# A two-layer hybrid trunk in float32: branch and output products as pairs of 512 and 256 columns, in a written order

## The chip, the cores and the metric

The kernel runs on one core of one Trainium2 chip. A core has a matrix engine (PE, with a row of its own, PEld, for loading weights), a vector engine (DVE), a scalar engine (ACT), a general engine (POOL) and a queue engine (SP) that here only starts transfers. PE writes its products to PSUM, a memory of eight banks; DVE and ACT read PSUM, POOL does not. The metric is the time on the device for one execution, in microseconds (us). Three timed runs of the kernel before took 999.44 us in the median (999.4 to 999.6). What a measurement of this kernel can tell from no change is about 0.2%, or 2 us.

## The reference

One sequence of 256 positions and 1024 channels goes through two layers. All arrays are float32.

```
x = x + 0.5 * swiglu(rms_norm(x), ...)              # first FFN, hidden width 2816
h = rms_norm(x);  z = h @ w_in                       # u | q | k | v | gates
y_pool = per-group map of (causal window means of u minus u) * scale
y_attn = causal attention over q, k, v (one block of 256 positions)
gates  = sigmoid(gl + b_gate)                        # two gates per output channel
merged = gates[0] * (y_pool @ w_branch_pool) + gates[1] * (y_attn @ w_branch_attn)
x = x + merged @ w_out
x = x + 0.5 * swiglu(rms_norm(x), ...)              # second FFN
```

The change concerns the last lines of the middle part: the two **branch** products, the gated sum `merged`, the **output** product with `w_out`, the sum into `x`, and what the second FFN needs of the new `x`.

## The kernel before, in words

**Exact products.** Every float32 operand is split into a high part, rounded to the matrix engine's float32r format, and a low part, the rest. A product is the sum of three: high by high, high by low, low by high. A weight block of 128 by 128 meets an activation tile of 128 channels by 256 positions, held as its two parts side by side (2 x 256 columns). There are two ways to write a block:

- `chain` (a **pair**): the high weights meet both parts in one product of 512 columns, then the low weights meet the high part in one product of 256 columns, added onto the first half. The result has two halves of 256 columns in PSUM, which must be added afterwards.
- `chain3` (a **triple**): three products of 256 columns, all added in the same 256 columns of PSUM. Nothing is left to add.

**Weights.** They stream from memory in units of 1 MB (two halves of 128 x 1024). SP starts a unit's transfer into one of four raw buffers; for each half ACT copies the raw data to `hi` (line 122) and DVE subtracts to get `lo` (line 123). There are six buffers each for `hi` and `lo`, so three units may stand ready. `request()` issues one whole unit, and `unit()` hands out the next.

**The middle of a layer.** After attention and the last two gate pairs, PE computes 64 branch blocks (eight output groups f of 128 channels, for each four blocks of the pooled branch and four of the attention branch), then 64 output blocks (eight groups of eight), then goes straight on with the second FFN. In the branch part, `mixed(f)` multiplies the two branch sums by the gates, adds them and splits the result `mg` into the parts `mk[f]` that the output product reads. Groups f = 2, 3, 4 (the set `wide`) are pairs: ACT copies each second half out of PSUM and DVE adds the first half to it, four instructions for the two branches, and POOL makes the sum of the two branches. The other five groups are triples, and DVE reads their PSUM tile directly. In the output part, groups 0 to 3 are pairs: ACT copies the second half, POOL adds `x`, DVE adds the first half. Groups 4 to 7 are triples with a single DVE addition. The output part starts groups 0, 1, 2 on the first six `mk`, then adds the last two.

**After each output group.** `after(f)` calls `prep`: ACT and DVE split the new `x` times a gain into `hx[f]`, the input parts of the second FFN, and ACT squares `x`, which DVE sums in `acc` for the norm. PE's first products of the FFN read `hx[0]`, `hx[1]` and so on. A little later PE sums `acc` over the channels with two products by ones (`ss`), for which `acc` is first split into `ar`.

**What sets the order.** Each engine runs its own instructions strictly in the order of its list, and waits in place. A scheduler of the framework writes these lists when the program is built. Instructions passed through `keep` stay in the order in which the code has them; PE's all are. DVE's and ACT's in the branch and output parts are not, so there the scheduler chose their order.

**The end.** The last FFN's last output group (22 blocks) is all triples, so that only one DVE instruction (line 451) stands between the last product and the last store.

Of the kernel before, what the change touches and what calls it, by code (L numbers as in the profile page):

```python
# [24 lines left out]
P = 128  # L25
D = 1024
S = 256
# [22 lines left out]
def trunk_kernel(ctx: ExitStack, tc: tile.TileContext, x_in, w_in, pw_in, qkn_in, rope_in, mask_in, band_in, out):  # L50
# [182 lines left out]
    nc.gpsimd.memset(uT[:, :, :PAD], 0.0)  # L233
# [8 lines left out]
    keep(nc.gpsimd.dma_start(gx[:, L * NG + 2 * S:L * NG + 4 * S], x_in[:, L * NG + 2 * S:L * NG + 4 * S]))  # L242

# [19 lines left out]
    def prep(f, l, col):  # L263
        split_x(f, l, col)
        square_x(f)
# [45 lines left out]
    def ffn(after, n0=0, end=False):  # L311
# [52 lines left out]
        for b in range(NK * NF):  # L364
# [5 lines left out]
            if f < NK - 1 or not end:  # L370
                chain(ps, hi, lo, b % 16, gs[k], k == 0, k == NF - 1)
            else:
                chain3(ps[:, 0, :], hi, lo, b % 16, gs[k:k + 1], k == 0, k == NF - 1)
# [71 lines left out]
    def add_x(f, ps, two):  # L445
# [120 lines left out]
    def mix(l, after):  # L566
# [26 lines left out]
        def open_gate(f):  # L593
            tt(gates[:, f], gates[:, f], bc2(r), op=OP.mult)
            for j in range(2):
                c = j * NK + f
                act(gates[:, f, j, :], gates[:, f, j, :], AF.Tanh, scale=0.5, bias=hb[:, c:c + 1])
# [137 lines left out]
        gate(7)  # L735
        open_gate(7)
        mt = acts.tile([P, NK, 2, S], F32R, name="mk", tag="ga")
        mk = [mt[:, i] for i in range(NK)]

        def branch(f, j, k0=0, k1=4):  # L740
            if f not in sums:
                sums[f] = quarter("two")
            if f in wide:
                for k in range(k0, k1):
                    chain(sums[f][j], *ws[f // 2], f % 2 * 8 + j * 4 + k, (pk, yk)[j][k], k == 0, k == 3)
            else:
                chain3(sums[f][:, j], *ws[f // 2], f % 2 * 8 + j * 4 + k0, (pk, yk)[j][k0:k1], k0 == j == 0,
                       j == 1 and k1 == 4)

        def mixed(f):  # L750
            mg = tmp.tile([P, 2, S], F32, name="mg", tag="t512", bufs=5)
            both = sums[f]
            if f in wide:
                both = mg
                for i in range(2):
                    act(mg[:, i, :], sums[f][i][:, 1, :], AF.Copy)
                    tt(mg[:, i, :], sums[f][i][:, 0, :], mg[:, i, :], op=OP.add)
            stt(mg, gates[:, f], 1.0, both, op0=OP.add, op1=OP.mult)
            (nc.gpsimd.tensor_tensor if f in wide else tt)(mg[:, 0, :], mg[:, 0, :], mg[:, 1, :], op=OP.add)
            halves(mk[f], mg[:, 0, :])  # L760

        ws = [unit() for _ in range(2)]
        sums = {f: quarter("two") for f in range(2)}
        wide = range(2, 5)
        sums.update({f: banks(pmm, "two") for f in range(2, 4)})
        sums = {f: [z[:, j] for j in range(2)] if f in wide else z for f, z in sums.items()}
        sums[4] = [quarter("two") for _ in range(2)]
        for f in range(4):
            for j in range(2):
                branch(f, j, 0, 2)  # L770
        for f in range(4):
            for j in range(2):
                branch(f, j, 2)
            mixed(f)
        for f in range(4, NK):
            if f % 2 == 0:
                ws.append(unit())
            for j in range(2):
                branch(f, j)
            mixed(f)  # L780
        ws, sums = [], []

        def project(f, k0=0, k1=NK):
# [5 lines left out]
            if f >= 4:  # L789
                chain3(ps[:, 0], *ws[f // 2], f % 2 * 8 + k0, mk[k0:k1], k0 == 0, k1 == NK)  # L790
            else:
                for k in range(k0, k1):
                    chain(ps, *ws[f // 2], f % 2 * 8 + k, mk[k], k == 0, k == NK - 1)
# [141 lines left out]
```

## Time and profile before

| | us |
|---|---|
| median of three timed runs | 999.44 |
| profiled execution, its own time | 999.57 |
| span of the profiled execution | 997.6 |
| PE, DVE, ACT, POOL busy | 993.6, 799.5, 628.7, 17.5 |
| branch part of layer 1, layer 2 (start to start of the output part) | 280.00 to 301.90, 774.1 to 796.0 |

The span covers all work that the profile shows; 2.0 us of the profiled execution's time lie around it. Each view below is of that one execution. In a timeline a row gives start, duration, engine, source line, operation, the tile that is written and the tiles that are read, the shape, how many like it follow at once, and in brackets how long the engine had been idle and what released it. On DVE and ACT an instruction may start some 0.08 us before the one ahead of it has ended, so the distance from start to start is what a row of instructions costs.

### The profile page before, as it was taken

What the parts mean: (1) busy time and instruction counts of PE and PEld (TensorE: products, weight loads), DVE (VectorE), ACT (ScalarE), POOL (GpSimd) and SP (SyncE); (2) the same over time, 40 slices, a digit from 0 to 9 for tenths busy, and PEclk for the clock granted to TensorE, in tenths of its full rate; (3) what the DMA queues carried; (4) which work ended last, traced back from release to release, by engine and by line L of the source; (5) the groups of instructions that cost most, each with busy time, mean ns of one, the idle gap of its engine ahead of it and who ended that gap; (6) DMA issues with size and microseconds to landing.
All of it is one profiled execution on the core that took longest, in us unless ns stands there. A gap on an engine that the chain in (4) does not pass through costs nothing.

```text
span 997.6 us, 15761 instructions
## 1 busy us (share of the span) xinstructions
PE 993.6 (100%) x6220; PEld 899.1 (90%) x6220; DVE 799.5 (80%) x1183; ACT 628.7 (63%) x999; POOL 17.5 (2%) x53
## 2 busy tenths in 40 slices
PE   9999999999999999999999999999999999999998
PEld 8998888898899988988898898888989999889888
DVE  7987786799879988886688888667998799888752
ACT  7766565657866766655576666556678567656541
POOL 1000000000001000000000000000000010000000
PEclk9999999999999999999999999999999999999999
DMA  9655565643536655655556566555545266555640
GB/s 314 243 207 209 194 245 214 220 170 120 219 127 211 214 208 182 204 207 204 181 193 215 178 211 205 182 204 191 193 151 194 100 235 216 198 204 189 211 143 27
DMA packets 30154, 192.88 MB, mean 193 GB/s; under 512 B 3360, under 2 KB 5408, under 8 KB 7552
## 3 DMA queue, kind: packets, MB, share of 16 engines
q1 hardware_dynamic: 29664, 191.18, 55.0%
q8 instruction: 48, 0.79, 0.3%
q0 software_dynamic: 128, 0.39, 0.1%
q10 hardware_dynamic: 288, 0.31, 0.1%
q14 instruction: 26, 0.21, 0.1%
HBM read 190.82 MB, written 1.05 MB: 192 GB/s over the span
## 4 chain that ended last, share of the span: by engine, by line
PE 100%; DVE 0%; issue 0%
PE ps L80 85%; PE pt L80 6%; PE two L80 4%; PE at L80 2%; PE pe L80 1%; PE at L546 1%; PE busy L80 0%; PE tp L507 0%; PE ss L80 0%; DVE gx L451 0%
## 5 line engine op out<-in xcount | busy, mean ns | idle before, releaser
L80 PE MATMUL ps<-hx,hi 128*128 128x512 f32 (+1 forms) x1714 | 572.2, 383 | 0.0
L123 DVE TENSOR_TENSOR lo<-raw,hi 128x1024 fp32r<-128x1024 f32 (+2 forms) x333 | 393.9, 1189 | 115.3 <-ACT hi L122 110.6
L80 PE MATMUL ps<-hx,lo 128*128 128x256 f32 x1712 | 464.6, 273 | 0.0
L122 ACT ACTIVATE hi<-raw 128x1024 fp32r<-128x1024 f32 (+2 forms) x333 | 339.6, 1029 | 190.4 <-PE ps L80 153.9
L80 PEld LDWEIGHTS ps<-hx,hi 128*128 128x128 f32 x1714 | 321.1, 188 | 56.8 <-issue 0.3
L80 PEld LDWEIGHTS ps<-hx,lo 128*128 128x128 f32 x1712 | 321.2, 188 | 0.8
L80 PE MATMUL ps<-ga,hi 128*128 128x512 f32 (+1 forms) x264 | 87.0, 376 | 0.0
L80 PE MATMUL ps<-gc,hi 128*128 128x512 f32 (+1 forms) x264 | 87.0, 376 | 0.0
L80 PE MATMUL ps<-ga,lo 128*128 128x256 f32 x256 | 69.9, 273 | 0.0
L80 PE MATMUL ps<-gc,lo 128*128 128x256 f32 x256 | 69.9, 273 | 0.0
L80 PE MATMUL ps<-gb,hi 128*128 128x512 f32 (+1 forms) x198 | 65.6, 376 | 0.0
L80 PE MATMUL pt<-hi,hx 128*128 128x512 f32 x192 | 64.3, 382 | 0.0
L80 PEld LDWEIGHTS ps<-ga,hi 128*128 128x128 f32 x264 | 49.0, 188 | 8.3
L80 PEld LDWEIGHTS ps<-gc,hi 128*128 128x128 f32 x264 | 49.0, 188 | 8.3
L80 PE MATMUL pt<-lo,hx 128*128 128x256 f32 x192 | 52.5, 273 | 0.0
L80 PE MATMUL ps<-gb,lo 128*128 128x256 f32 x192 | 52.4, 273 | 0.0
L190 DVE TENSOR_TENSOR ab<-ps,ab 128x512 f32<-128x512 f32 x56 | 38.6, 688 | 16.2 <-ACT ab L189 14.9
L80 PEld LDWEIGHTS ps<-ga,lo 128*128 128x128 f32 x256 | 48.1, 188 | 0.0
L80 PEld LDWEIGHTS ps<-gc,lo 128*128 128x128 f32 x256 | 48.1, 188 | 0.0
L388 DVE TENSOR_TENSOR lo<-raw,hi 128x1024 fp32r<-128x1024 f32 x38 | 44.7, 1217 | 0.0
L80 PE MATMUL two<-yp,hi 128*128 128x256 f32 (+1 forms) x208 | 43.9, 301 | 0.0
L80 PE MATMUL ps<-mk,hi 128*128 128x256 f32 (+1 forms) x192 | 43.5, 311 | 0.0
(162 smaller groups left out, 1130.1 us busy)
## 6 DMA issues: line engine op xcount, KB each, us to landing
raw<-w SPq DMA_DIRECT2D x176, 1024.0 KB, 4.9
raw<-w SPq DMA_DIRECT2D x6, 256.0 KB, 6.0
raw<-w SPq DMA_DIRECT2D x11, 128.0 KB, 3.8
raw<-w SPq DMA_DIRECT2D x2, 512.0 KB, 6.1
gx<-x SPq DMA_DIRECT2D x2, 256.0 KB, 5.7
qk<-pw SPq DMA_DIRECT2D x2, 256.0 KB, 3.3
out_dram<-gx SPq DMA_DIRECT2D x2, 256.0 KB, 2.7
out_dram<-gx SPq DMA_DIRECT2D x1, 384.0 KB, 5.4
```

What stands on the lines that cost most here:

```text
L80: return keep(nc.tensor.matmul(*args, **kw))
L122: put(act(hi, w, AF.Copy))
L123: put(tt(lo, w, hi.bitcast(F32), op=OP.subtract))
L190: put(tt(t, ps[:, :, 0, :], t, op=OP.add))
L388: keep(tt(lo[h], raw[:, h * HALF:(h + 1) * HALF], hi[h].bitcast(F32), op=OP.subtract))
L546: keep(nc.tensor.transpose(line(pt)[:, j * P:(j + 1) * P], pr[:, h, c * P:(c + 1) * P], ident))
```

## The change

1. All 64 branch blocks and all 64 output blocks are pairs. `branch` and the set `wide` are gone. For every group two PSUM tiles are taken, alternately from the two pools. ACT copies two second halves, DVE adds two first halves, and the sum of the two branches, before on POOL for three groups, is on DVE for all eight.
2. In the output part every group has ACT copy the second half, DVE add the first half to `x`, and DVE add the copy. POOL's four additions per layer are gone.
3. The order of ACT and DVE in these parts is written out with `keep`, `prep` included. Weights are split half a unit at a time by `next_half()`: after branch groups 0, 1, 2, 4 and 6, three halves after the last group, one half after each of output groups 0 to 5, and two at the end. Three units are requested ahead, behind the last gate pair's products.
4. The last gate pair is drained at once, but its scaling and its two activations (`open_gate(7)`) come after branch group 3.
5. The last group of the last FFN has 17 blocks as pairs in one PSUM tile, which is added to `x` with the usual three instructions (`add_x`), and five blocks as triples in a second tile, added with one.
6. The padding columns of `uT` are cleared one column at a time, on POOL, behind POOL's second input transfer instead of ahead of it.

```diff
-    nc.gpsimd.memset(uT[:, :, :PAD], 0.0)
...
+    for t in range(PAD):
+        keep(nc.gpsimd.memset(uT[:, :, t:t + 1], 0.0))
...
             if f < NK - 1 or not end:
                 chain(ps, hi, lo, b % 16, gs[k], k == 0, k == NF - 1)
+            elif k < NF - 5:
+                chain(ps, hi, lo, b % 16, gs[k], k == 0, k == NF - 6)
             else:
-                chain3(ps[:, 0, :], hi, lo, b % 16, gs[k:k + 1], k == 0, k == NF - 1)
+                if k == NF - 5:
+                    add_x(f, ps)
+                    ps = quarter("ps")
+                chain3(ps[:, 0, :], hi, lo, b % 16, gs[k:k + 1], k == NF - 5, k == NF - 1)
...
+        def next_half():
+
+            if not begun:
+                raw = raws.tile([P, 2 * HALF], F32, name="raw", tag="raw")
+                nc.sync.dma_start(raw, w_in[n_unit[0]])
+                n_unit[0] += 1
+                begun.append((raw, [], []))
+            raw, hi, lo = begun[0]
+            h = len(hi)
+            hi.append(parts.tile([P, HALF], F32R, name="hi", tag="hi"))
+            lo.append(parts.tile([P, HALF], F32R, name="lo", tag="lo"))
+            split(raw[:, h * HALF:(h + 1) * HALF], hi[h], lo[h], keep)
+            if h:
+                begun.clear()
+                ahead.append((hi, lo))
...
+        def mixed(f, ps):
+
             mg = tmp.tile([P, 2, S], F32, name="mg", tag="t512", bufs=5)
...
+                keep(act(mg[:, j, :], ps[j][:, 1, :], AF.Copy))
             for j in range(2):
+                keep(tt(mg[:, j, :], ps[j][:, 0, :], mg[:, j, :], op=OP.add))
+            keep(stt(mg, gates[:, f], 1.0, mg, op0=OP.add, op1=OP.mult))
+            return mg
...
             for j in range(2):
-                branch(f, j)
-            mixed(f)
+                for k in range(4):
+                    chain(ps[j], *ws[f // 2], f % 2 * 8 + j * 4 + k, (pk, yk)[j][k], k == 0, k == 3)
+            mgs.append(mixed(f, ps))
+            if f:
+                halves(mk[f - 1], mgs[f - 1][:, 0, :], keep)
+            keep(tt(mgs[f][:, 0, :], mgs[f][:, 0, :], mgs[f][:, 1, :], op=OP.add))
+            if f == 3:
+                open_gate(7, keep)
+            if f in (0, 1, 2, 4, 6):
+                next_half()
+        halves(mk[-1], mgs[-1][:, 0, :], keep)
+        for _ in range(3):
+            next_half()
...
-            if f >= 4:
-                chain3(ps[:, 0], *ws[f // 2], f % 2 * 8 + k0, mk[k0:k1], k0 == 0, k1 == NK)
-            else:
-                for k in range(k0, k1):
-                    chain(ps, *ws[f // 2], f % 2 * 8 + k, mk[k], k == 0, k == NK - 1)
+            for k in range(k0, k1):
+                chain(ps, *ws[f // 2], f % 2 * 8 + k, mk[k], k == 0, k == NK - 1)
             if k1 == NK:
-                t = x[:, f, :]
-                if f < 4:
-                    t = small.tile([P, S], F32, name="t", tag="sg", bufs=2)
-                    act(t, ps[:, 1, :], AF.Copy)
-                    nc.gpsimd.tensor_tensor(t, t, x[:, f, :], op=OP.add)
-                tt(x[:, f, :], ps[:, 0, :], t, op=OP.add)
+                t = small.tile([P, S], F32, name="t", tag="sg", bufs=2)
+                keep(act(t, ps[:, 1, :], AF.Copy))
+                keep(tt(x[:, f, :], ps[:, 0, :], x[:, f, :], op=OP.add))
+                keep(tt(x[:, f, :], x[:, f, :], t, op=OP.add))
+                if f < 6:
+                    next_half()
                 after(f)
...
+        for _ in range(2):
+            next_half()
...
-        mix(l, lambda f: prep(f, l, C_G2))
+        mix(l, lambda f: prep(f, l, C_G2, keep))
```

**How it moves instructions.** The first place is DVE's list in the branch part of the first layer. `two` is a PSUM tile of branch sums, `gates` holds the gates, `mg` a group's gated sums, `mk` the parts for the output product, and `lo` the low parts of weights. Before, groups 0 to 2 and the beginning of 3:

```order
L758 SCALAR_TENSOR_TENSOR mg_3022<-gates_2128,two_2964 128x512
L759 TENSOR_TENSOR mg_3022<-mg_3022 128x256
L123 TENSOR_TENSOR lo_3146<-raw_3143,hi_3144 128x1024
L206 TENSOR_TENSOR mk_2953<-mg_3022,mk_2953 128x256
L758 SCALAR_TENSOR_TENSOR mg_3039<-gates_2128,two_2965 128x512
L123 TENSOR_TENSOR lo_3147<-raw_3143,hi_3145 128x1024
L759 TENSOR_TENSOR mg_3039<-mg_3039 128x256
L757 TENSOR_TENSOR mg_3052<-two_2966,mg_3052 128x256
L123 TENSOR_TENSOR lo_3216<-raw_3213,hi_3214 128x1024
L206 TENSOR_TENSOR mk_2953<-mg_3039,mk_2953 128x256
L757 TENSOR_TENSOR mg_3052<-two_2966,mg_3052 128x256
L757 TENSOR_TENSOR mg_3069<-two_2967,mg_3069 128x256
```

And with the change, at the same place, groups 0 and 1 and the beginning of 2:

```order
L771 TENSOR_TENSOR mg_3004<-two_2986,mg_3004 128x256
L771 TENSOR_TENSOR mg_3004<-two_2987,mg_3004 128x256
L772 SCALAR_TENSOR_TENSOR mg_3004<-gates_2143,mg_3004 128x512
L789 TENSOR_TENSOR mg_3004<-mg_3004 128x256
L123 TENSOR_TENSOR lo_3014<-raw_3011,hi_3013 128x1024
L771 TENSOR_TENSOR mg_3034<-two_3017,mg_3034 128x256 x2
L772 SCALAR_TENSOR_TENSOR mg_3034<-gates_2143,mg_3034 128x512
L206 TENSOR_TENSOR mk_2985<-mg_3004,mk_2985 128x256
L789 TENSOR_TENSOR mg_3034<-mg_3034 128x256
L123 TENSOR_TENSOR lo_3044<-raw_3011,hi_3043 128x1024
L771 TENSOR_TENSOR mg_3065<-two_3047,mg_3065 128x256
L771 TENSOR_TENSOR mg_3065<-two_3048,mg_3065 128x256
```

Every group now has two additions from PSUM (L771) ahead of its product with the gates (L772), the parts `mk` of a group come one group later, and a `lo` stands at a fixed place after a group's sum.

The second place is DVE's list at the end of the output part, up to the split of the norm's sums. `gx` holds `x`, `hx` the input parts of the second FFN, `acc` the sum of squares, `ar` its parts, and `hold` the first up-projection results. Before, from output group 6's sum of squares on:

```order
L261 TENSOR_TENSOR acc_156<-acc_156,sq_3445 128x256
L123 TENSOR_TENSOR lo_3590<-raw_3587,hi_3588 128x1024
L800 TENSOR_TENSOR gx_79<-ps_3448,gx_79 128x256
L123 TENSOR_TENSOR lo_3591<-raw_3587,hi_3589 128x1024
L252 SCALAR_TENSOR_TENSOR hx_155<-gx_79,hx_155 128x256
L261 TENSOR_TENSOR acc_156<-acc_156,sq_3476 128x256
L123 TENSOR_TENSOR lo_3633<-raw_3630,hi_3631 128x1024
L206 TENSOR_TENSOR ar_3555<-acc_156,ar_3555 128x256
```

With the change, from group 6's sum into `x` on:

```order
L810 TENSOR_TENSOR gx_79<-ps_3425,gx_79 128x256
L811 TENSOR_TENSOR gx_79<-gx_79,t_3442 128x256
L253 SCALAR_TENSOR_TENSOR hx_170<-gx_79,hx_170 128x256
L262 TENSOR_TENSOR acc_171<-acc_171,sq_3448 128x256
L810 TENSOR_TENSOR gx_79<-ps_3451,gx_79 128x256
L811 TENSOR_TENSOR gx_79<-gx_79,t_3468 128x256
L253 SCALAR_TENSOR_TENSOR hx_170<-gx_79,hx_170 128x256
L262 TENSOR_TENSOR acc_171<-acc_171,sq_3474 128x256
L123 TENSOR_TENSOR lo_3480<-raw_3477,hi_3479 128x1024
L123 TENSOR_TENSOR lo_3484<-raw_3477,hi_3483 128x1024
L190 TENSOR_TENSOR hold_3490<-ps_3491,hold_3490 128x512
L206 TENSOR_TENSOR ar_3543<-acc_171,ar_3543 128x256
```

Between the last sum of squares and `ar` there stood one `lo` before; now there stand two and the drain of the FFN's first product (L190).

More of the change, by code (lines that the diff above doesn't have):

```diff
@@ L261, in square_x, with prep @@
             put(tt(acc, acc, sq, op=OP.add))
-    def prep(f, l, col):
-        split_x(f, l, col)
-        square_x(f)
+    def prep(f, l, col, put=lambda i: i):
+        split_x(f, l, col, put)
+        square_x(f, put)
     def rsqrt(r, ss, inv):
@@ L443, in in_order, with add_x @@
         request((), keep)
-    def add_x(f, ps, two):
+    def add_x(f, ps, two=True):
         t = x[:, f, :]
@@ L591, in gate, with open_gate @@
             pair(unit(), gates[:, f], *other)
-        def open_gate(f):
-            tt(gates[:, f], gates[:, f], bc2(r), op=OP.mult)
+        def open_gate(f, put=lambda i: i):
+            put(tt(gates[:, f], gates[:, f], bc2(r), op=OP.mult))
             for j in range(2):
                 c = j * NK + f
-                act(gates[:, f, j, :], gates[:, f, j, :], AF.Tanh, scale=0.5, bias=hb[:, c:c + 1])
+                put(act(gates[:, f, j, :], gates[:, f, j, :], AF.Tanh, scale=0.5, bias=hb[:, c:c + 1]))
         def project_u():
@@ L734, in mix @@
             map_end(2 + p, ats[2 + p])
-        gate(7)
-        open_gate(7)
+        last = sum_pair(unit())
+        for _ in range(3):
+            request()
+        drain(gates[:, 7], last, keep)
         mt = acts.tile([P, NK, 2, S], F32R, name="mk", tag="ga")
         mk = [mt[:, i] for i in range(NK)]
[L740 to L743, printed above, removed]
-                for k in range(k0, k1):
-                    chain(sums[f][j], *ws[f // 2], f % 2 * 8 + j * 4 + k, (pk, yk)[j][k], k == 0, k == 3)
-            else:
-                chain3(sums[f][:, j], *ws[f // 2], f % 2 * 8 + j * 4 + k0, (pk, yk)[j][k0:k1], k0 == j == 0,
-                       j == 1 and k1 == 4)
@@ L750, in mixed @@
-        def mixed(f):
-            mg = tmp.tile([P, 2, S], F32, name="mg", tag="t512", bufs=5)
[L752 to L768, printed above, removed]
+        begun = []
+        def next_half():
[12 more added lines that the diff above has]
+                ahead.append((hi, lo))
@@ L769, in mix @@
+        def mixed(f, ps):
+            mg = tmp.tile([P, 2, S], F32, name="mg", tag="t512", bufs=5)
             for j in range(2):
-                branch(f, j, 0, 2)
-        for f in range(4):
+                keep(act(mg[:, j, :], ps[j][:, 1, :], AF.Copy))
             for j in range(2):
-                branch(f, j, 2)
-            mixed(f)
-        for f in range(4, NK):
+                keep(tt(mg[:, j, :], ps[j][:, 0, :], mg[:, j, :], op=OP.add))
+            keep(stt(mg, gates[:, f], 1.0, mg, op0=OP.add, op1=OP.mult))
+            return mg
@@ L776, in mix @@
+        ws, mgs = [], []
+        for f in range(NK):
             if f % 2 == 0:
                 ws.append(unit())
+                ps = [quarter("two") for _ in range(2)]
+            else:
+                ps = banks(pmm, "two")
+                ps = [ps[:, j] for j in range(2)]
             for j in range(2):
-                branch(f, j)
-            mixed(f)
+                for k in range(4):
[8 more added lines that the diff above has]
+                next_half()
@@ L781, in mix @@
+        halves(mk[-1], mgs[-1][:, 0, :], keep)
+        for _ in range(3):
+            next_half()
         ws, sums = [], []
```

2 lines of the change are left out of this document (removed).

## The prediction

> **What bounds the kernel now.** I read the page first, then the chain of waits in order of time, then the engines by stretch around the changed parts, then the timelines of single engines there.
>
> ```profile
> span 997.6 us, 15761 instructions
> PE 993.6 (100%) x6220; PEld 899.1 (90%) x6220; DVE 799.5 (80%) x1183; ACT 628.7 (63%) x999; POOL 17.5 (2%) x53
> PE 100%; DVE 0%; issue 0%
> ...
> 280.16 21.90 PE two L80 x168
> 302.06 29.70 PE ps L80 x208
> 331.75 0.23 PE ss L80 x2
> 331.99 176.02 PE ps L80 x1056
> ...
> 774.27 21.90 PE two L80 x168
> ```
>
> PE is the bound from end to end: the chain never leaves it. So a product saved is time saved, and any wait of PE is time lost. The row of 331.99 prices a pair: 1056 products are 528 pairs in 176.02 us, 333.4 ns each. But the slack is thin:
>
> ```profile
> 280.16:302.06 21.90, 21.90 (x170) 21.00 (x169) 16.58 (x29) 13.64 (x24) 2.45 (x3) 1.00 0.29 97
> 302.06:324.00 21.94, 21.94 (x163) 20.83 (x163) 20.11 (x34) 14.09 (x26) 4.80 (x4) 1.00 0.70 240
> 324.00:331.75 7.75, 7.75 (x49) 6.98 (x49) 7.07 (x12) 5.37 (x9) 0.00 (x0) 1.00 0.67 225
> ```
>
> After its length, a row gives PE, PEld, DVE, ACT, POOL busy. From the branch part to `ss`, DVE works 43.8 of 51.6 us, and in the output part 20.1 of 21.9. This change adds work to DVE there.
>
> **What PE gains.** A triple's price and a pair's in the branch part:
>
> ```profile
> 280.00 0.39 PE L80 MATMUL two<-yp,hi 128*128 128x256 f32 x2
> ...
> 282.41 0.40 PE L80 MATMUL two<-yp,hi 128*128 128x256 f32 x2
> ...
> 288.18 0.38 PE L80 MATMUL two<-yp,hi 128*128 128x512 f32 x1
> ...
> 290.23 0.38 PE L80 MATMUL two<-yp,hi 128*128 128x512 f32 x1
> ```
>
> The first two rows start triples seven apart: 2.41/7 = 344 ns. So a triple turned into a pair saves 11 ns. Five branch groups of eight blocks and four output groups of eight are 72 blocks a layer, 144 in two, and 17 in the last block: 161 x 10.9 ns = 1.76 us. The last two rows start pairs six apart: 2.05/6 = 342 ns, so pairs in this stretch run slow. Why is not visible; 16 per layer do. They stand behind a run of triples, and none is left there, so I count them at 333: 32 x 8.3 ns = 0.27 us. **Gain 2.0 us**; if all branch pairs run at 342 it is 128 x 8.3 + 0.27 = 1.3 less, 0.7.
>
> The Trainium skill ("TensorE: Matmul & The Clock Gate", Back-to-back issue gap) has a product cost its columns plus some 2.5 ns. By that a triple is only one fixed cost dearer than a pair, and the 161 blocks would save an estimated 0.4 us. The rows show 11 ns a block, so the trace disagrees, and the measured number stands.
>
> **What DVE must do instead.** Start-to-start prices come from rows like these:
>
> ```profile
> 282.32 0.68 DVE L190 TENSOR_TENSOR gates<-ps,gates 128x512 f32<-128x512 f32 x1
> 286.99 0.69 DVE L758 SCALAR_TENSOR_TENSOR mg<-gates,two 128x512 f32<-128x512 f32 x1 [3.26 <-PE two L80]
> 287.72 0.43 DVE L759 TENSOR_TENSOR mg<-mg 128x256 f32<-128x256 f32 x1
> ...
> 303.74 0.68 DVE L758 SCALAR_TENSOR_TENSOR mg<-gates,two 128x512 f32<-128x512 f32 x1
> 304.34 1.22 DVE L123 TENSOR_TENSOR lo<-raw,hi 128x1024 fp32r<-128x1024 f32 x1
> 305.48 0.42 DVE L206 TENSOR_TENSOR mk<-mg,mk 128x256 fp32r<-128x256 f32 x1
> 305.81 0.42 DVE L759 TENSOR_TENSOR mg<-mg 128x256 f32<-128x256 f32 x1
> ...
> 320.35 0.74 DVE L800 TENSOR_TENSOR gx<-ps,gx 128x256 f32<-128x256 f32 x2
> 321.02 1.21 DVE L123 TENSOR_TENSOR lo<-raw,hi 128x1024 fp32r<-128x1024 f32 x1
> 322.15 0.47 DVE L252 SCALAR_TENSOR_TENSOR hx<-gx,hx 128x256 fp32r<-128x256 f32 x1
> 322.55 0.41 DVE L261 TENSOR_TENSOR acc<-acc,sq 128x256 f32<-128x256 f32 x1
> 322.88 0.47 DVE L252 SCALAR_TENSOR_TENSOR hx<-gx,hx 128x256 fp32r<-128x256 f32 x1
> ```
>
> An addition of 256 columns costs 0.33, a product or drain of 512 0.60, a weight half 1.14, an `hx` 0.40. An instruction that reads the result just ahead of it starts 0.04 after its end (287.72): then an addition costs 0.46 and a product 0.72. The new sum `gx<-gx,t` has no row of its own; `mg<-mg`, also from SBUF alone, has 0.42 of duration, the same.
>
> A branch group now costs DVE 0.33 + 0.46 + 0.60 + 0.33 + 0.33 = 2.05 (two additions, gates, `mk` of the group before, sum). With a weight half it is 3.19, and PE needs only 8 x 0.333 = 2.67. An output group costs 0.46 + 0.33 + 1.14 + 0.40 + 0.33 = 2.66, as much as PE: what lag the branch part leaves is carried to the end.
>
> ACT adds waits, since the written order makes it alternate with DVE:
>
> ```profile
> 276.31 0.91 ACT L597 ACTIVATE gates<-gates,hb 128x256 f32<-128x256 f32 x2 [0.21 <-DVE gates L594]
> ...
> 306.26 0.42 ACT L205 ACTIVATE mk<-mg 128x256 fp32r<-128x256 f32 x1 [1.99 <-DVE mg L759]
> ...
> 309.64 0.64 ACT L798 ACTIVATE t<-ps 128x256 f32<-128x256 f32 x2
> ...
> 317.54 0.51 ACT L251 ACTIVATE hx<-gx 128x256 fp32r<-128x256 f32 x1 [2.44 <-DVE gx L800]
> 317.95 0.41 ACT L260 ACTIVATE sq<-gx 128x256 f32<-128x256 f32 x1
> ...
> 328.12 1.05 ACT L122 ACTIVATE hi<-raw 128x1024 fp32r<-128x1024 f32 x1
> ```
>
> DVE's clock for layer 1, from the drain of the last gate pair (282.32 + 0.60 = 282.92):
> - group 0 without `mk`: 1.84; groups 1 to 7: 7 x 2.05 = 14.35; five halves: 5.70; the last gates' scaling: 0.60. Waits: 0.30 for group 1's copies (PE ends at 285.5, two copies 0.64), 1.35 in group 4, where ACT does both activations (0.91) and a copy first. That is 307.06. The last `mk` waits 0.56 for ACT's half and costs 0.34: 307.96.
> - three halves, the first 0.65 late behind ACT's `hi`: 312.03.
> - output groups 0 to 5: 2.33 (no sum of squares) + 5 x 2.66 = 327.66. Group 6 has no half to fill the wait for ACT's `hx`: 0.79 + 0.65 + 0.73 = 329.83. Group 7: 0.79 + 0.65, so `hx[7]` runs from 331.27 to 331.75.
>
> PE's clock: branch 280.00 + 64 x 0.3334 = 301.34. `mk[5]`, needed at 303.0, ends at 303.65: stall 0.7. Output ends at 301.34 + 0.68 + 21.34 = 323.36. The FFN takes `hx[5]` at 326.69 and gets it at 327.41 (0.72), `hx[6]` 1.5 late, `hx[7]` 0.2 late. Together **3.1 us**.
>
> Then the norm. Before, its parts came in time for `ss` at 331.75:
>
> ```profile
> 328.42 0.47 DVE L252 SCALAR_TENSOR_TENSOR hx<-gx,hx 128x256 fp32r<-128x256 f32 x1
> ...
> 330.34 0.42 DVE L206 TENSOR_TENSOR ar<-acc,ar 128x256 fp32r<-128x256 f32 x1
> ```
>
> Now `ar` stands behind two weight halves and a drain: after `hx[7]` 331.67 + 0.33 (`acc`), 0.56 waiting for `hi`, 2 x 1.14, 0.60, 0.42 = 335.86. PE is there six pairs after `hx[7]`, at 333.78, and its second `ss` product could start at 333.89: stall **2.0 us**.
>
> So 5.1 us a layer; the second layer has the same order and the same times 494.1 us later (774.27 against 280.16). Two layers: 10.2. Bounds: DVE's path here is 53 us, and 2% on its prices moves the stall by 1.0 a layer either way: 4.1 to 6.1. What DVE's lag delays beyond `ss` (the factor r, the next drains) has cover, since DVE has a fifth of the FFN free.
>
> **What costs nothing.** The last group's 17 blocks are added under five triples, 5 x 0.344 = 1.72 us; the three instructions took 1.36 from start to end in the group before:
>
> ```profile
> 986.82 0.39 ACT L449 ACTIVATE t<-ps 128x256 f32<-128x256 f32 x1 [6.95 <-PE ps L80]
> 987.23 0.43 DVE L450 SCALAR_TENSOR_TENSOR t<-t,gx 128x256 f32<-128x256 f32 x1 [6.01 <-ACT t L449]
> 987.76 0.42 DVE L451 SCALAR_TENSOR_TENSOR gx<-ps,t 128x256 f32<-128x256 f32 x1
> ```
>
> Uncovered they would cost at most 1.4. The padding columns lie on POOL behind its last input transfer, and `uT` is read only in the middle of a layer; that transfer starts one clearing earlier.  POOL's sums cost PE nothing before.
>
> **Sum.** 999.57 - 2.0 + 10.2 = 1007.8 in the profile's own terms. The median lies 0.13 below the profiled execution: **1007.6 us**.
>
> **Rivals.**
> - *DVE keeps up* (7%). If DVE's real lag at `hx[5]` were 3.1 us smaller, and `ar` were in time, only the gain is left: 997.4. For it: before, POOL's sums slowed DVE beside them, which now ends, and DVE's durations overlap. Against: the prices above are from undisturbed rows and are start to start, and 2.05 and 3.19 against 2.67 leave no room. It decides when DVE's path is some 10% shorter than my sum.
> - *Only the norm stalls* (5%). The lag is filled by the waits I counted against DVE, and `hx` comes in time; `ar` alone then costs 2.0 a layer: 999.44 - 2.0 + 4.0 = 1001.4.
> - *The lag runs on* (6%). If the FFN's third up-projection also waits, because the PSUM tile of the first is drained late behind the halves, one drain and one half (1.7 us) a layer come on top: 1011.
> - The forecast holds with 82%.
>
> **How the numbers follow.** Around the forecast, 4.1 to 6.1 us of stall a layer is 1005.6 to 1009.6; a gain of only 0.7 adds 1.3. For lesser errors of the clocks I widen that to **1005.0 to 1010.5**; the rivals outside hold under 2 in 10. A measurement of this kernel can tell 0.2%, 2 us, from no change. Faster by more: 5%, most of the first rival; within: 4%, the rest of it and part of the second; slower: 91%.
>
> **What would show it.** In the changed profile: PE rows with idle time ahead of `ps<-mk` near 303, of `ps<-hx` at `hx[5]` and `hx[6]` near 327 to 330, and of `ss`; `ss` some 4 us later after the branch start than the 51.7 us of before; DVE busy nearly all the time from 283 to 331; pairs at 333 ns in the branch part, and the last group as short as 17 x 0.333 + 5 x 0.344. It is wrong if `ss` comes 51 us after the branch start, or if PE waits in places that this clock doesn't have, above all for weights.

## The result

| | before | changed |
|---|---|---|
| median | 999.54 us (6 runs) | 1013.36 us (6 runs) |
| single executions | 999.4 to 999.8 | 1008.66, 1012.83, 1013.32, 1013.39, 1017.53, 1017.75 |
| profiled execution, its own time and its span | 999.57, 997.6 | 1008.66, 1006.8 |

The ratio is 1.0143 [1.0124, 1.0162]: slower. Ratios here and below leave out an execution more than 1.5% above the fastest of its kernel; the only one is the 1023.86 us of the first repeat, whose granted clock (0.997) lies within that of the others (0.996 to 1.000). The six executions of the changed kernel don't lie in one place but on three steps, some 4.5 us apart. The forecast was 1007.6 us, with a range up to 1010.5. The lowest step lies within it, the median 2.9 us above it.

The profile is of an execution on the lowest step. First its page (span, busy times), which answers to the lines shown of before:

```profile
span 1006.8 us, 15509 instructions
PE 997.1 (99%) x6059; PEld 894.6 (89%) x6059; DVE 815.3 (81%) x1227; ACT 636.6 (63%) x1028; POOL 3.6 (0%) x54
```

DVE has 15.8 us more to do, POOL 13.9 less. The chain of waits, in order of time (start, length, what it went through):

```profile
280.26 5.35 PE two L80 x32
309.91 2.35 DVE lo L123 x2
...
332.73 2.36 DVE lo L123 x2
336.55 176.00 PE ps L80 x1056
...
778.81 5.35 PE two L80 x32
...
835.10 168.06 PE ps L80 x1013
```

Before, this chain never left PE. Now it runs over DVE's weight halves in both layers. From the branch start to the pairs behind `ss` it takes 336.55 - 280.26 = 56.29 us, before 331.99 - 280.16 = 51.83: 4.46 more, and the same in layer 2 (835.10 - 778.81). That makes 8.9 of the 9.1 us by which this execution is longer. The last group saves 0.2; the start takes 0.1 and the program's end some 0.3 more.

PE's timeline at the waits of layer 1:

```profile
302.98 0.27 PE L80 MATMUL ps<-mk,lo 128*128 128x256 f32 x1
303.86 0.49 PE L80 MATMUL ps<-mk,hi 128*128 128x512 f32 x1 [0.60 <-DVE mk L206]
...
327.63 0.50 PE L80 MATMUL ps<-hx,hi 128*128 128x512 f32 x1 [0.51 <-DVE hx L253]
...
328.31 0.28 PE L80 MATMUL ps<-hx,lo 128*128 128x256 f32 x1
329.83 0.49 PE L80 MATMUL ps<-hx,hi 128*128 128x512 f32 x1 [1.24 <-DVE hx L253]
...
331.29 0.63 PE L80 MATMUL ps<-hx,hi 128*128 128x512 f32 x1
...
331.93 0.63 PE L80 MATMUL ps<-hx,hi 128*128 128x512 f32 x1
...
336.17 0.38 PE L80 MATMUL ss<-ar,one_r 128*128 128x256 f32 x1 [0.28 <-DVE ar L206]
```

The brackets give the idle time of PE's array. What a wait costs is read from the starts: 302.98 to 303.86 are 0.87 us (the rows are rounded), where a 256-column product takes 0.11, so 0.76. The waiting product itself is 0.11 longer than the others (0.49 against 0.38), so this wait costs 0.76 + 0.11 = 0.87 us in all. Counted so, the four waits of layer 1 come to 0.87, 0.79, 1.51 and 0.55 us. In between, from 331.29 to 331.93, a pair takes 0.64 us instead of 0.33: PE's clock is at half there. The stretches show it (length, then PE, PEld, DVE, ACT, POOL busy, then PE's granted clock):

```profile
280.26:301.60 21.34, 21.34 (x129) 19.20 (x129) 18.65 (x35) 12.20 (x27) 0.00 (x0) 1.00 0.32 105
326.60:336.55 9.95, 7.93 (x35) 6.33 (x34) 8.07 (x16) 6.45 (x13) 0.00 (x0) 0.83 0.39 115
336.55:512.55 176.00, 176.00 (x1058) 158.34 (x1058) 138.53 (x191) 108.38 (x161) 0.00 (x0) 1.00 0.58 203
```

The first row is the branch part: 64 pairs in 21.34 us, 333.4 ns each. The second has the mean clock 0.83. The slow stretch cost nothing extra, because PE waited at its end for `ar` anyway: in the run with a break below, the same stretch from branch start to the pairs behind `ss` takes 56.19 us in a layer whose clock is whole and 56.23 us in one whose clock is at half for a while. The last row is the FFN at 333 ns a pair. So this execution shows where 9.1 us went, but not where the median's other 4.7 come from.

### The profile page after: what moved, and what is told of

Its sections match the earlier page's. It is cut to its first block, busy times and chain, and to the rows that moved or that the text cites. A ratio compares the mean times of both kernels' runs of the same rounds, so it can differ in the third digit from the quotient of the medians.

```text
span 1006.8 us, 15509 instructions
## 1 busy us (share of the span) xinstructions
PE 997.1 (99%) x6059; PEld 894.6 (89%) x6059; DVE 815.3 (81%) x1227; ACT 636.6 (63%) x1028; POOL 3.6 (0%) x54
## 4 chain that ended last, share of the span: by engine, by line
PE 90%; DVE 8%; ACT 1%; issue 1%; DVEq 0%
PE ps L80 79%; PE pt L80 6%; DVE lo L123 3%; PE at L80 1%; PE two L80 1%; DVE mg L771 1%; DVE mg L772 1%; DVE hx L253 1%; DVE gx L810 1%; PE pe L80 1%; PE at L552 1%; DVE mg L789 1%; DVE gx L811 0%; DVE acc L262 0%; ACT hi L122 0%
## 5 line engine op out<-in xcount | busy, mean ns | idle before, releaser
L80 PE MATMUL ps<-gc,hi 128*128 128x512 f32 x256 | 86.9, 382 | 0.0
L80 PE MATMUL ps<-ga,hi 128*128 128x512 f32 x256 | 86.9, 382 | 0.0
L190 DVE TENSOR_TENSOR ab<-ps,ab 128x512 f32<-128x512 f32 x56 | 38.6, 689 | 16.2 <-ACT ab L189 14.9
L80 PE MATMUL ps<-mk,hi 128*128 128x512 f32 x128 | 43.1, 384 | 1.2 <-DVE mk L206 1.2
L80 PE MATMUL two<-yp,hi 128*128 128x512 f32 x128 | 42.8, 382 | 0.0
```

The costliest lines, as they stand in the source:

```text
L80: return keep(nc.tensor.matmul(*args, **kw))
L190: put(tt(t, ps[:, :, 0, :], t, op=OP.add))
```

## The experiments

"Levels" are single executions, sorted. In the expectations of the first four runs, theory A is that the stretches at half clock make the steps; in all later ones, that a wait leaves the pairs behind it slow.

### The changed kernel again

No edit.

> The changed kernel itself, nothing edited, to see how its executions are spread and to get a second trace. Theory A (PE's waits for the vector engine cost a fixed 4.3 us a layer, and on top of it they sometimes let the granted clock fall to a half for windows of 3.4 us, whose cost depends on where a window falls): executions between 1008 and 1018 us, in steps rather than a smear; the trace shows the same waits at the same places within 0.1 us, and where it is slower, half-clock stretches that no wait covers. Theory B (the spread has nothing to do with PE's waits, such as transfers that land late): the trace shows waits for transfers or another length of DVE's work.

Measured: 1012.68 us (1008.69, 1008.86, 1012.68, 1013.20, 1023.86), ratio 1.0112 [1.0096, 1.0128]. The profile caught the slowest. The chain of waits, the two rows that answer to 336.55 and 835.10 above:

```profile
336.68 186.54 PE ps L80 x1056
...
845.87 172.50 PE ps L80 x1013
```

The same 1056 products take 10.5 us longer in layer 1 and 1013 products 4.4 longer in layer 2, without one wait. PE's timeline in the middle of layer 1's second FFN, some 65 us after the last wait:

```profile
400.11 0.40 PE L80 MATMUL ps<-hx,hi 128*128 128x512 f32 x1
...
400.46 0.39 PE L80 MATMUL ps<-hx,hi 128*128 128x512 f32 x1
...
400.81 0.40 PE L80 MATMUL ps<-hx,hi 128*128 128x512 f32 x1
```

Two pairs start 0.70 us apart, 353 ns on the mean of the FFN. And the stretches of both FFNs:

```profile
336.68:523.20 186.52, 186.52 (x1059) 161.15 (x1058) 138.77 (x191) 107.51 (x161) 0.00 (x0) 1.00 0.56 191
845.87:1018.35 172.48, 172.48 (x1013) 152.44 (x1012) 123.73 (x167) 92.84 (x134) 0.00 (x0) 1.00 0.50 170
```

PE is busy throughout and its clock is whole (1.00). So an FFN has a persistent **pitch** (the time from the start of one pair to the start of the next): 333, 342 or 353 ns. The 353 ns stand in this one execution alone, the slowest. With 528 pairs the steps are 528 x 9 = 4.75 and 528 x 20 = 10.5 us. One or two layers at 342 ns added to the lowest level give the levels near 1013.2 and 1017.7; of those two the changed kernel has no profile.

### Products that fill the waits

Products that nobody reads are put where PE waited: three ahead of `mk[5]` and of `hx[5]`, six ahead of `hx[6]`, sixteen of 256 columns ahead of `ss`.

```
+            for _ in range(fills.get(k, 0)):
+                prod(room[:, 0], blk(w[0], 0), hk[k - 1], True, True)
...
+        for _ in range(n):
+            prod(z[:, 1], w, hk[3][:, 0], True, True)
```

> The changed kernel with useless products on PE in the places where it waits: 3 of 512 columns ahead of mk[5], 3 ahead of hx[5], 6 ahead of hx[6], 16 of 256 columns ahead of the sums ss, all into PSUM that is free, so that PE works instead of waiting and every wait keeps its end. Theory A: with no idle stretch the clock stays at 1.00, the waits cost what they cost by DVE's clock alone, and all executions lie at 1007 to 1009.5 us, within 1 us of each other. Theory B: the spread stays, 1008 to 1018. If the products themselves cost time, all executions are later by up to 12 x 0.22 + 16 x 0.11 = 4.4 us a layer, but together.

Measured: 1015.3 us (1009.27, 1013.04, 1013.06, 1017.55, 1017.92, 1021.67), ratio 1.0158 [1.0128, 1.0188]. The stretch that had half clock above:

```profile
326.60:336.55 9.95, 9.95 (x61) 8.45 (x60) 8.29 (x16) 7.27 (x14) 0.00 (x0) 1.00 0.40 117
```

Busy products keep the clock at 1.00, and the steps are all still there. The half clock doesn't make them; theory A of this group falls. The executions of the changed kernel say the same: its 1008.66 has a mean clock of 0.996, its 1017.5 and 1017.8 have 1.000.

This profile (of the 1013.06) shows more. From the branch start to the pairs behind `ss` its layers take 56.18 and 56.31 us, as without the fills, and then one of its two FFNs is slow, 4.4 us longer than 168.06:

```profile
336.27 176.00 PE ps L80 x1056
...
835.05 172.49 PE ps L80 x1013
```

What stands ahead of the slow FFN, in layer 2:

```profile
832.83 2.00 PE L80 MATMUL ss<-hx,hi 128*128 128x256 f32 x16
834.66 0.40 PE L80 MATMUL ss<-ar,one_r 128*128 128x256 f32 x2
834.89 0.38 PE L80 MATMUL ps<-hx,hi 128*128 128x512 f32 x1
```

Eighteen products take 2.06 us, 114 ns each, as in a triple (344 / 3) that waits for nothing. The last four pairs ahead of them (831.16 to 832.49) are at 333 ns, the pairs behind at 342. So no wait stands at this `ss`, and still the FFN is slow: a wait there is not needed. Ahead of the pairs there is a long run of products of 256 columns, as in a triple, and before the change 16 pairs behind triples stood at 342 ns too; whether the run is the cause here was not tested.

### `ar` ahead of the last two weight halves

```
+        early.append(factor_parts(keep))
         for _ in range(2):
             next_half()
...
-            r.append(factor_end(factor_sums(factor_parts())))
+            r.append(factor_end(factor_sums(early.pop() if early else factor_parts())))
```

> The changed kernel with the split of the sum of squares (ar) moved ahead of the two last weight halves on ACT and DVE. By the prediction's clock this takes 2.0 us a layer away: the clock-free time is 1008 - 4 = 1004 us. Theory A: executions from 1004 us up, with a spread of several us still, since the waits for hx[5] and hx[6] are left; where the clock falls, its 1.7 us are now uncovered, so the fastest may be at 1004 to 1007.5. Theory B: 1004 to 1014 as well, but with the clock at 1.00. If the wait for ar was not real: no gain, 1008 to 1018.

Measured: 1005.73 us (1004.84 to 1006.27, 4 runs), ratio 1.0063 [1.0048, 1.0077]. PE's waits in this kernel (total, times, longest):

```profile
PE ps L80 <- DVE hx L253: 3.5, 4, 1.2
PE ps L80 <- DVE mk L206: 1.2, 2, 0.6
```

The wait for `ar` is gone, those for `mk` and `hx` are as they were. The profiled execution is 3.8 us under the lowest of the changed kernel, about the predicted 2 x 2.0. And no execution lies a step of 4 us higher, although four waits for `hx` remain: with an `ss` that doesn't wait behind them, they left no FFN slow in these four.

### Only the last group in 17 and five blocks

The kernel before with this part of the change alone.

```
+            elif k < NF - 5:
+                chain(ps, hi, lo, b % 16, gs[k], k == 0, k == NF - 6)
             else:
-                chain3(ps[:, 0, :], hi, lo, b % 16, gs[k:k + 1], k == 0, k == NF - 1)
+                if k == NF - 5:
+                    add_x(f, ps)
+                    ps = quarter("ps")
+                chain3(ps[:, 0, :], hi, lo, b % 16, gs[k:k + 1], k == NF - 5, k == NF - 1)
```

> The kernel before with the change's fifth part alone: 17 of the last group's 22 blocks as pairs, five as triples in a second PSUM tile. By the prediction 17 x 10.9 ns = 0.19 us faster, 999.3 us, the three instructions of add_x being covered by the five triples. If the cover fails, up to 1.4 us slower; if pairs and triples cost the same, no change.

Measured: 999.4 us (11 runs) against 999.57, ratio 0.9998 [0.999, 1.0007]. The size fits 17 x 10.9 ns = 0.19 us but can't be told from nothing.

### A late `ss` in the kernel before

Nothing of the change; the sum of squares takes six more steps on DVE that leave it as it is.

```
+            for _ in range(late):
+                tt(acc, acc, acc, op=OP.max)
             r.append(factor_end(factor_sums(factor_parts())))
...
-            ffn(lambda f: prep(f, l + 1, C_G1))
+            ffn(lambda f: prep(f, l + 1, C_G1), late=6)
...
-            ffn(store, end=True)
+            ffn(store, end=True, late=6)
```

> The kernel before with nothing of the change: only the sum of squares is passed six times through max(acc, acc) on VectorE ahead of `ar`, which leaves its values as they are and makes it some 2 us later. `ss` then waits for `ar` for an estimated 1.1 us in each layer (six reads of a just written tile at 0.46 us, less the 1.0 us by which `ar` came early and 0.6 us that overlaps). Theory A (a wait of TensorE can leave the pairs behind it slow until the next break in the run of pairs): 999.5 + 2 x 1.1 = 1001.7 in some executions, and in others 4.5 to 10.5 us more, with pairs at 342 or 353 ns after `ss`. Theory B (the slow pairs belong to the pair form of the branch and output products, or to VectorE's load there): every execution within 1 us of 1001.7, all pairs after `ss` at 333 ns.

Measured: 1007.59 us (1004.43, 1005.97, 1007.59, 1007.78, 1007.98), ratio 1.0068 [1.0055, 1.0081]. The wait is longer than meant: the rows ahead of and at `ss`, and the stretches before and behind it:

```profile
331.89 0.27 PE L80 MATMUL ps<-hx,lo 128*128 128x256 f32 x1
333.89 0.84 PE L80 MATMUL ss<-ar,one_r 128*128 128x256 f32 x2 [1.72 <-ACT ar L205]
```

```profile
331.70:334.90 3.20, 1.40 (x8) 0.86 (x7) 2.56 (x6) 1.48 (x3) 0.00 (x0) 1.00 0.40 166
334.95:338.36 3.41, 3.41 (x14) 2.87 (x12) 3.12 (x5) 3.02 (x4) 0.00 (x0) 0.52 0.26 50
```

Of 3.20 us PE was idle for 1.80, and for the next 3.41 us the clock is at half, which costs 1.7 us. Here that explains all: 1004.4 with no such stretch (mean clock 1.000), 1006.0 with one (0.998), 1007.6 to 1008.0 with two (0.997). No FFN was left slow in the execution profiled. So this run gives no support to theory A, though PE waited right ahead of the FFN in both layers, and its expectation missed the wait by about 1.2 us a layer.

### A break behind the waiting `ss`

The changed kernel with two products of 256 columns that nobody reads, four pairs behind `ss`, in the two FFNs that follow the changed parts (`reset` is 2 there and 0 elsewhere).

```
-            columns(ws[1], pss[1], range(4, NK))
+            columns(ws[1], pss[1], range(4, 6))
+            if reset:
+                spare = quarter("spare")[:, 0]
+                for _ in range(reset):
+                    prod(spare, blk(ws[1][0], 0), hk[0][:, 0], True, True)
+            columns(ws[1], pss[1], range(6, NK))
```

> The changed kernel with two products of 256 columns more in each layer, four pairs behind the `ss` that waits; they go into a PSUM tile that nobody reads and wait for nothing. They cost 2 x 0.11 us a layer. Theory A (a wait leaves the pairs slow, and the next break in the run of pairs, such as an `ss` that doesn't wait, sets them back to 333 ns): all executions at 1008.7 + 0.5 = 1009.2, at most 1 us more for the pairs between the wait for `mk` and that for `hx`. Theory B (what makes the pairs slow holds for the whole stretch, whatever products stand in it): the same spread as the changed kernel, 1009 to 1024, with a median near 1013.

Measured: 1009.15 us (1008.81, 1009.08, 1009.22, 1009.57), ratio 1.0095 [1.0082, 1.0108]. All four lie where the lowest step is; of the changed kernel's eleven executions eight lie some 4 us or more above it. (The repeat of the changed kernel ran on another chip than this one; the two orders without triples below, with and without a break, ran on the same.)

### Two other written orders

Both have the last gates' activations behind group 5, `ar` ahead of the last weight half, and fewer halves between the branch and the output part. One turns output groups 5 and 6 back into triples, the other has no triples. The diff is that of the second; the first has halves behind groups 0, 1, 2, 4 and 6 and two behind the branch part.

```
             if f == 3:
-                open_gate(7, keep)
-            if f in (0, 1, 2, 4, 6):
+                keep(tt(gates[:, 7], gates[:, 7], bc2(r), op=OP.mult))
+            if f == 5:
+                for j in range(2):
+                    c = j * NK + 7
+                    keep(act(gates[:, 7, j, :], gates[:, 7, j, :], AF.Tanh, scale=0.5, bias=hb[:, c:c + 1]))
+            if f in (0, 1, 2, 4, 6, 7):
                 next_half()
         halves(mk[-1], mgs[-1][:, 0, :], keep)
-        for _ in range(3):
+        for _ in range(1):
             next_half()
...
+        early.append(factor_parts(keep))
-        for _ in range(2):
+        for _ in range(1):
             next_half()
```

> The changed kernel with another written order: the last gates' activations behind group 5 instead of group 3, two of the weight halves behind the branch part instead of three, `ar` ahead of the last half, one half there instead of two, and output groups 5 and 6 back in triples, which take one PSUM read on VectorE instead of two additions. By the durations of the traces no product waits between the branch part and `ss`. It gives up 16 blocks a layer x 10.9 ns = 0.17 us, and the pairs behind the triples may run at 342 ns (0.1 us). Theory A: 997.4 + 0.3 to 0.6 = 998.0 in all executions, without a spread, since there is no wait. Rival: pairs in the written order are worth nothing, 999.4.

Measured: 999.08 us (998.61 to 1000.19, 11 runs), ratio 0.9996 [0.9987, 1.0004]: no wait of PE between the branch part and the FFN, no steps, and not to be told from before. The expected 998.0 was missed by 1 us; in its profile the 31 pairs from 319.98 to 330.59 behind the triples stand at 342 ns in each layer, 0.6 us in two, and the program's end takes the 0.3 us more that the changed kernel has too.

> The same without triples in branch and output part: all blocks as pairs, six halves inside the branch part, one behind it, one behind `ar`. By the durations of the traces one product of `hx[7]` waits 0.25 us a layer. By the length of the wait alone: 997.4 + 0.5 = 997.9. Theory A: that in some executions, and others with up to 9 us more, if so short a wait already leaves the pairs slow. Rival: a short wait doesn't, and all executions lie within 1 us.

Measured: 1001.53 us, ratio 1.0025 [1.0005, 1.0045]. Levels: six executions at 999.1 to 999.6, four at 1003.5 to 1004.1, two at 1008.2 and 1008.8. The profiled one is of the middle level. The chain's rows for the two FFNs:

```profile
331.70 176.07 PE ps L80 x1055
...
825.48 172.54 PE ps L80 x1012
```

Layer 1 is at 333 ns a pair, layer 2 at 342. What stands in front of each row, on PE's timeline:

```profile
331.05 0.39 PE L80 MATMUL ps<-hx,hi 128*128 128x512 f32 x1
331.70 0.38 PE L80 MATMUL ps<-hx,lo 128*128 128x256 f32 x1 [0.27 <-DVE lo L123]
...
824.59 0.39 PE L80 MATMUL ss<-ar,one_r 128*128 128x256 f32 x2
824.83 0.38 PE L80 MATMUL ps<-hx,hi 128*128 128x512 f32 x1
825.48 0.38 PE L80 MATMUL ps<-hx,lo 128*128 128x256 f32 x1 [0.27 <-DVE lo L123]
```

`ss` is in time. The one wait is of 0.43 us (824.83 to 825.48, less 0.22), for the last weight half and not, as I had written, for `hx[7]`. So behind a wait of 0.43 us an FFN can be 4.5 us longer; by the times of the twelve executions it was in 8 of 24 layers. Layer 1 of this execution waited as long (331.05 to 331.70) and its pairs ran at 333 ns: the same wait goes with either pitch. The expectation of 997.9 was 1.2 us or more too low even for the lowest level: the wait cost 0.54 us a layer with the longer product behind it instead of 0.25, and the 0.3 us at the program's end were not in it.

### The break in the order without triples

The same two idle products, behind the product that waits for its weights.

> The reordered kernel without triples, and in each layer two products of 256 columns more, into a PSUM tile that nobody reads, four pairs behind `ss` and behind the product that waited 0.4 us for its weights. They cost 2 x 2 x 0.11 = 0.5 us. Theory A (a wait leaves the pairs slow, and a break in the run of pairs sets them back): the 4.5 us steps are gone, every execution at 999.4 + 0.5 = 999.9, within 0.6 us. Theory B (the break does nothing): about half of the executions 4 to 9 us above that, as without the break.

Measured: 999.57 us, all twelve executions between 999.36 and 999.92, ratio 0.9996 [0.9988, 1.0005]. Six of twelve stood 4 us or more higher without the two products, none of twelve with them: 0.4 us of products save 2 us in the median. The wait for `lo` is still in the profile.

### Triples in the last two output groups

The order with two triples, moved to groups 6 and 7, and the weight halves as in the order without triples.

```
-            if f in (5, 6):
+            if f in (6, 7):
                 chain3(ps[:, 0], *ws[f // 2], f % 2 * 8 + k0, mk[k0:k1], k0 == 0, k1 == NK)
```

> The reordered kernel with output groups 6 and 7 in triples instead of 5 and 6, so that only the pairs ahead of `ss` and none of an output group stand behind triples; six halves inside the branch part, one behind it, one behind `ar`. By the durations of the traces nothing waits, and the last weight half is 0.6 us ahead of its first product. If the pairs behind triples run at 342 ns only until `ss`: 998.9 - 2 x 0.2 = 998.5 in all executions, without steps. Rival: a triple is itself what sets the pitch, and the steps or the slow pairs are back: 999 to 1004.

Measured: 999.07 us (998.75 to 999.99, 12 runs), ratio 0.9992 [0.9984, 1.0001]. No steps. The 23 pairs from the triples to `ss` (323.14 to 331.01) are at 342 ns in both layers, those behind `ss` at 333. So here two products that don't wait, those of `ss`, set a slow pitch back. It is the best order tried, 0.6 us under before in the medians, and not told from it.

### Where the wait stands

Two more delays in the kernel before: three steps of `max` ahead of both halves of `ar`, so that the **first** `ss` product waits; and four steps between its two halves, so that the **second** waits.

> The kernel before with the sum of squares passed three times through max(acc, acc) instead of six, so that the first `ss` product waits some 1.0 us a layer, too short to bring the half clock: 999.6 + 2.0 = 1001.6. Six passes gave 1004.4 where the clock stayed whole, and no slow run of pairs was seen. Theory A1 (any wait of TensorE just ahead of the pairs can leave them slow): some executions 4.5 or 9 us higher. Theory A2 (a wait at the first `ss` product does not, since the second `ss` product behind it is itself the break; a wait behind the break is needed): all executions within 1 us of 1001.6.

> The kernel before with the four passes through max(acc, acc) put between the two halves of `ar`, so that the first `ss` product is in time and the second waits some 1.1 us: 999.6 + 2.2 = 1001.8. Theory A1 (any wait): some executions 4.5 or 9 us higher. Theory A2 (a wait that is behind the last break, as that of the second `ss` product): the same, in a good part of the executions, where the wait at the first `ss` product gives none. If neither kernel has steps, what makes the pairs slow is more than a wait.

PE's rows at `ss`, first of the one, then of the other:

```profile
331.74 0.27 PE L80 MATMUL ps<-hx,lo 128*128 128x256 f32 x1
332.37 0.84 PE L80 MATMUL ss<-ar,one_r 128*128 128x256 f32 x2 [0.35 <-ACT ar L205]
```

```profile
331.67 0.27 PE L80 MATMUL ss<-ar,one_r 128*128 128x256 f32 x1
332.75 0.38 PE L80 MATMUL ss<-ar,one_r 128*128 128x256 f32 x1 [0.80 <-DVE ar L292]
```

Measured with the first late: 1001.56 us, ratio 1.002 [1.001, 1.003], eleven of twelve executions between 1001.3 and 1002.3 and one at 1006.2. With the second late: 1005.81 us, ratio 1.0049 [1.0033, 1.0066], two of eight at 1001.6 and six at 1005.3 to 1007.1. The delay costs about 2 us in both, as meant; the step of some 4 us comes in 1 of 12 against 6 of 8. The profiles are of executions without a step.

The two kernels differ in more than the place of the wait. With the first product late the second one waits too: the two take 0.84 us in the first row of `ss`, where two that don't wait take 0.39, so their starts lie 0.46 us apart instead of 0.11. The second product then waits 0.35 us in the one kernel and 0.97 in the other. A wait of 0.43 us brought the step in half the executions above, so length alone is not an easy explanation, but this pair of runs doesn't tell place from length. What it does show is that a late `ss` alone, with nothing else of the change, brings the steps: in 6 of 8 executions, where the kernel before has 2 of 88.

### The late second product again, and with a break

> The kernel before with the four passes through max(acc, acc) between the two halves of `ar`, once more, for its profile. 6 of 8 executions stood 4 to 5 us above the other two. Theory A (pairs left slow by the wait of the second `ss` product): an execution near 1005.7 has, in one of its layers, all pairs from `ss` to the next break at 342 ns, 4.5 us longer than 176.0 (or 168.1) us, and nothing else longer. Rival: the 4.2 us lie elsewhere, for example in the weights' transfers or in the start.

Measured: 1001.46, 1001.74, 1006.33, ratio 1.0038 [1.0019, 1.0056]. The profile is of the 1001.74, without a step, so it settles nothing.

> The same kernel with two products of 256 columns more, four pairs behind the `ss` that waits, into a PSUM tile that nobody reads. Theory A: no steps, every execution at 1001.6 + 2 x 2 x 0.11 = 1002.0, within 0.6 us. Rival (the step is a cost of the delay itself): most executions 4 us higher, as without the break.

Measured: 1002.68 us (1002.00 to 1003.61, 6 runs), ratio 1.0031 [1.0019, 1.0043]. No execution has the 4 us step (of the two runs without the break, on two chips, 7 of 11 have it; on this chip 1 of 3). They spread over 1.6 us instead of the 1.2 expected, their spans over 0.7 (1000.1 to 1000.8); in the profiled one (1003.29) 2.6 us lie outside the span, 0.6 more than before. Its timeline in layer 2:

```profile
828.53 0.38 PE L80 MATMUL ss<-ar,one_r 128*128 128x256 f32 x1 [0.79 <-DVE ar L292]
828.75 0.39 PE L80 MATMUL ps<-hx,hi 128*128 128x512 f32 x1
...
829.08 0.39 PE L80 MATMUL ps<-hx,hi 128*128 128x512 f32 x1
...
829.77 0.39 PE L80 MATMUL ps<-hx,hi 128*128 128x512 f32 x1
...
830.11 0.39 PE L80 MATMUL spare<-hx,hi 128*128 128x256 f32 x2
830.34 0.39 PE L80 MATMUL ps<-hx,hi 128*128 128x512 f32 x1
...
832.38 0.38 PE L80 MATMUL ps<-hx,hi 128*128 128x512 f32 x1
...
833.38 0.38 PE L80 MATMUL ps<-hx,hi 128*128 128x512 f32 x1
```

Behind the waiting `ss` three pairs take 829.77 - 828.75 = 1.02 us, 340 ns each. Behind the break six pairs take 832.38 - 830.34 = 2.04, still 340 ns each, and then three take 833.38 - 832.38 = 1.00, 333 ns each, and so it stays to the end of the FFN. Layer 1 shows the same course. But the kernel before, whose `ss` waits for nothing, has pairs like these behind it:

```profile
331.82 0.39 PE L80 MATMUL ps<-hx,hi 128*128 128x512 f32 x1
...
332.85 0.38 PE L80 MATMUL ps<-hx,hi 128*128 128x512 f32 x1
```

Three pairs in 1.03 us. So this profile doesn't show a slow pitch that the break ended; that the break works here is seen in the times only.

## Why the prediction was right and where it failed

- **Gain, 2.0 us: right.** The 64 branch pairs ran at 333.4 ns; the slow pairs in the branch part, behind triples, are gone with the triples.
- **DVE's clock: right.** Its last `mk` started at 307.82 (predicted 307.62), `hx[7]` at 331.48 (331.27), `ar` at 335.70 (335.44).
- **The stalls: right in place and nearly in size.** Predicted for `mk[5]`, `hx[5]`, `hx[6]`: 0.7, 0.72, 1.5; measured 0.87, 0.79, 1.51, in part since each waiting product is itself 0.11 longer. `hx[7]` (0.2) and `ss` (2.0) were measured as 0.55 at `ss` and 1.7 lost to the half clock ahead of it, which took the place of the wait. A layer lost 5.4 us against 5.1. The profiled execution has 1008.66 where the sum, in its terms, gave 1007.8.
- **The last group and POOL: right.** The chain's last row is 168.06 us, before 168.27, and the run of that part alone is 0.2 us faster, which can't be told from nothing; no wait of PE names POOL.
- **The step that failed** is the price of what comes behind a stall. The sum counted a wait only as its length and let the FFN behind `ss` keep its 333 ns a pair (the row of 176.02 us). The slow pairs of before, at 342 ns, were seen, put down with "Why is not visible", and counted as 0.27 us in the one place where they stood. The runs show in its place that with a late `ss`, or a wait just behind it, all pairs that follow can stand at 342 ns, once at 353, to the end of the FFN: 4.5 us a layer, once 10.5. The `ss` that waits is the last break ahead of 528 pairs, so that a stall at this very place is the dearest. By the times, one layer was slow in the median execution: 1008.7 + 4.5 = 1013.2, measured 1013.36. The profile at 1013.06 of the kernel with filled waits shows exactly that, one FFN at 342 ns and one at 333. That the profiled 1008.66 lies so near the forecast means that the waits were right and that it is an execution with no slow FFN.
- **The rivals.** "DVE keeps up" and "only the norm stalls" fell with the waits for `mk` and `hx`. "The lag runs on" gave 1011, the nearest figure, but by a wait that doesn't exist: the chain stays on PE from 336.55.

What is shown: the steps are runs of slow pairs (three profiles: the repeat, the filled waits, the order without triples); half clock is not their cause; a late second `ss` product alone brings them (by the times); they are gone when two products that wait for nothing stand behind the wait (three kernels, 22 executions) and when PE waits neither at `ss` nor behind it (three kernels, 27 executions), though the filled kernel, with no wait at the `ss` ahead of its slow FFN, has them in five of six. So a wait there is one way into the slow pitch, and not the only one. What stays open: by what inside PE the pitch is kept, why the same wait brings it in some layers only, whether a long run of products of 256 columns does it too, and whether two of 88 executions of the kernel before, which stand 4 us higher (1003.6 and 1003.9), had it.

## What to carry to other kernels

In a long run of equal products a wait may cost far more than its length, so look at the pitch of the products on both sides of it, and at several executions, before pricing it. Let no wait stand between the last product of another kind and a long run of pairs; if it can't be moved, two short idle products behind it are cheap. Filling the wait with idle products was no substitute here. When work is moved to an engine that has little slack, put what PE needs next (here `ar`) ahead of what it needs later (the weight halves).

## What the runs showed of the hardware

- **The pitch.** Pairs of 512 and 256 columns ran at 333 or 342 ns, in one execution at 353, with the clock at 1.00, and kept the pitch over some 500 pairs, through changes of the tiles read and written. It was slow behind a wait of 0.43 us in one layer and not behind an equal one in the other, and behind 18 products of 256 columns with no wait. Two products of 256 columns that waited for nothing (`ss`, triples in the last two output groups) set 342 back to 333 in both layers of one profile.
- **The clock** fell to half for 3.41 us after a stretch in which PE was idle for 1.80 of 3.20 us (late `ss` in the kernel before), and not after the single waits of 1.1 us (late second product). The Trainium skill ("TensorE: Matmul & The Clock Gate", What's actually happening) states a free-running window of 3413 ns and a halved clock after an idle one. The length agrees; the idle share differs, since here a window that was busy for over 40% was enough.
- **A product that waited** takes 0.11 us longer itself (0.49 against 0.38 us for 512 columns).
